# D's second projection units and A's units moved later in the mixer, with the conv's norm beside D's first half

## The chip, the cores and the metric

The kernel runs on one core of a Trainium2 chip. Its time is device time in microseconds of that core. Five engines work at once, each on its own queue in program order: TensorE (PE, with its weight loads PEld), VectorE (DVE), ScalarE (ACT), GpSimd (POOL) and SyncE (SP), which issues the transfers (DMA).

## The reference, cut to what matters

Two layers of a transformer block work on 512 latent tokens and, in layer 0, on 256 context tokens beside them (768 in all). Layer 1 gives out latents only. Each layer projects the normed tokens once, splits the columns into four groups, and computes:

```python
y_a = window_gqa(qa, ka, va, ka_c, va_c, sink)          # banded attention with a sink
y_b = conformer_conv(ub, conv_w, conv_b, conv_ln_g, conv_ln_b)   # conv of 31 taps, then layernorm and silu
y_c = diff_out(diff_attention_latent(qc, kc, vc, kc_c, vc_c, lam), subln_g, lambda_init)
y_d = neighbourhood_attn(qd, kd, vd, kd_c, vd_c, rpb)   # 2-D neighbourhood, with a bias
yx = jnp.concatenate([y_a, y_b, y_c, y_d], axis=-1) @ w_out
x = x + g1 * yx
x = x + g2 * swiglu(modulate(rmsnorm(x, norm2_g[l]), sh2, sc2), w_gate[l], w_up[l], w_down[l])
```

The shifts, scales and gates (`sh1` to `g2`) are six vectors of a layer, each a product of the conditioning with a part of `w_ada`. They are called ada vectors below, (layer, number); (1, 2) is the gate `g1` of layer 1. The context tokens of layer 0 go through the same groups among themselves.

## The kernel before

Every large product is made of three matmuls of split operands (`mm3`, L177 to L179: high by high, high by low, low by high), so a *unit* of 128 projected columns is 8 slices of the model width by 3 matmuls over 512 latent columns, and as many over 256 context columns where the group needs them. A unit's weights come by one load of 512 KB, ACT writes the high part (L142) and DVE the low part (L144).

The mixer of a layer (`layer`) is written as generators that hand out steps. `beside(main, side, nm, ns)` runs an attention half as main and spreads the steps of a side list between its steps, at a rate set by the two numbers; `mix2` and `chain` join lists; `take(g, n)` takes n steps of a list. From what is written, a scheduler of the framework makes each engine's queue, which runs in order. The attentions work by blocks of 128 queries: scores on TensorE (L630 and L631 for C and A, L794 for D) into one PSUM tile (`sc` or `sd`) that holds one block, a reduction on DVE (L662 for C, L805 for D, L855 for A), exponentials on ACT, for C a combining of two weights on DVE (L671), transposes of the weights on TensorE (L515, L516) and the product with the values (L621, L622). D's bias is written by POOL (L775).

The stages of a layer, in order:

- B's units, then the conv's taps on DVE (L880), which go on beside the stages that follow.
- C's first half, beside C's second queries and keys and D's first ones.
- C's second half, beside `d_rest`: D's second queries and keys (`proj_d(l, H, c1, 1)`), the rest of the taps, and D's two value units.
- D's first half, beside three of A's units (keys, values, first queries: `take(pa, 3)`).
- D's second half, beside `rest`: A's last unit (second queries), the release of the projection's input `hT`, the pool for `w_out`, A's mask, C's norm (`c_norm`) and the conv's layernorm (`conv_norm`: two transposes to rows per 128 tokens, statistics on DVE, a power on POOL, then transposes back and the silu).
- A, beside `more`: the first loads of `w_out` and the ada vector (l, 2), in layer 1 the ada vector first.

After the mixer come the product with `w_out` and the FFN, whose tiles hold TensorE for most of the time. In the FFN of layer 0 the ada vectors of later use are made beside it by a lazy list (`ada_half`): it loads 512 KB at a time, in pairs into two buffers (`araw`), and TensorE takes the loads in with small matmuls (L312). How many steps of that list run for each hidden tile f is a number in the loop (`for _ in range(10 if f < 1 else 2)`). A vector takes eight loads.

## Time and profile before

| | us |
|---|---|
| median of three runs (1778.98 to 1782.14) | 1779.81 |
| the profiled execution | 1780.37 |
| span of its profile | 1778.6 |
| TensorE busy | 1702.3 (96%) |
| VectorE busy | 935.1 (53%) |
| ScalarE busy | 584.9 (33%) |
| GpSimd busy | 205.8 (12%) |

The share of busy time is a mean over stages of different kinds: the FFN and the projections have TensorE full, the attention stages use all engines. So the profile is read by stage here, in stretches cut where a stage's first score reduction starts. In layer 0 the cuts stand at 109.9 us (C's first half), 197.1 (C's second), 266.1 (D's first), 300.0 (D's second), 339.0 (A) and 405.5 (first product with `w_out`); in layer 1 at 1123.6, 1185.3, 1236.5, 1274.8, 1293.2 and 1350.8. The row of a stretch gives its length, each engine's busy time in it with the number of instructions, the clock that TensorE was granted (1.00 is 2.4 GHz, 0.50 is 1.2), the mean busy share of the DMA engines and the bandwidth.

### The profile page before, as it was taken

What the parts mean: (1) busy time and instruction counts of PE and PEld (TensorE: products, weight loads), DVE (VectorE), ACT (ScalarE), POOL (GpSimd) and SP (SyncE); (2) the same over time, 40 slices, a digit from 0 to 9 for tenths busy, and PEclk for the clock granted to TensorE, in tenths of its full rate; (3) what the DMA queues carried; (4) which work ended last, traced back from release to release, by engine and by line L of the source; (5) the groups of instructions that cost most, each with busy time, mean ns of one, the idle gap of its engine ahead of it and who ended that gap; (6) DMA issues with size and microseconds to landing.
All of it is one profiled execution on the core that took longest, in us unless ns stands there. A gap on an engine that the chain in (4) does not pass through costs nothing.

```text
span 1778.6 us, 26995 instructions
## 1 busy us (share of the span) xinstructions
PE 1702.3 (96%) x11236; PEld 1413.5 (79%) x11236; DVE 935.1 (53%) x1548; ACT 584.9 (33%) x1048; POOL 205.8 (12%) x194
## 2 busy tenths in 40 slices
PE   6999999779999999999999999999988999999997
PEld 4888787557898888888888889878766888888886
DVE  5678875762452342423324258688565445354354
ACT  4225544562241112121121233454354422321221
POOL 1101113520000010000000010212440001000000
PEclk8999999888999999999999999999998999999999
DMA  9351122235155243242331212111225253432421
GB/s 323 83 170 36 36 57 68 72 91 180 44 164 173 85 120 109 70 123 95 97 97 37 86 69 71 49 48 35 90 62 178 73 177 95 119 90 76 119 71 48
DMA packets 187976, 172.78 MB, mean 97 GB/s; under 512 B 17878, under 2 KB 150478, under 8 KB 187726
## 3 DMA queue, kind: packets, MB, share of 16 engines
q1 hardware_dynamic: 187854, 171.06, 31.3%
q8 instruction: 88, 1.44, 0.3%
q14 instruction: 34, 0.28, 0.0%
HBM read 166.76 MB, written 4.52 MB: 96 GB/s over the span
## 4 chain that ended last, share of the span: by engine, by line
PE 85%; DVE 5%; DMA 4%; ACT 2%; SPq 1%; issue 1%; POOL 1%; POOLq 0%; DVEq 0%; ACTq 0%
PE ps L177 19%; PE ps L178 19%; PE ps L179 19%; PE pu L177 5%; PE pu L178 5%; PE pu L179 5%; PE sc L631 3%; PE pt L516 2%; PE pt L622 2%; PE ada L312 2%; SPq L98 1%; DMA wraw<-in_w_in 1%; PE pu L622 1%; DMA wraw<-in_w_gate 1%; PE ptd L516 1%
## 5 line engine op out<-in xcount | busy, mean ns | idle before, releaser
L178 PE MATMUL ps<-h,whi 128*128 128x512 f32 (+1 forms) x1104 | 382.5, 347 | 1.6 <-DVE h L144 1.6
L177 PE MATMUL ps<-h,whi 128*128 128x512 f32 (+1 forms) x1104 | 382.6, 349 | 0.9 <-DVE gt L985 0.9
L179 PE MATMUL ps<-h,wlo 128*128 128x512 f32 (+1 forms) x1104 | 381.9, 347 | 0.0
L142 ACT CAST whi<-wraw 128x1024 fp32r<-128x1024 f32 (+1 forms) x132 | 134.3, 1022 | 448.6 <-PE ps L178 250.6
L144 DVE TENSOR_TENSOR wlo<-wraw,whi 128x1024 fp32r<-128x1024 f32 (+1 forms) x116 | 139.2, 1203 | 186.4 <-ACT whi L142 185.3
L177 PEld LDWEIGHTS ps<-h,whi 128*128 128x128 f32 x1104 | 207.8, 189 | 30.0 <-issue 1.6
L178 PEld LDWEIGHTS ps<-h,whi 128*128 128x128 f32 x1104 | 209.0, 189 | 27.4 <-DVE h L144 2.0
L179 PEld LDWEIGHTS ps<-h,wlo 128*128 128x128 f32 x1104 | 208.8, 189 | 26.6 <-issue 0.6
L177 PE MATMUL ps<-wdhi,zh 128*128 128x512 f32 x440 | 171.4, 391 | 0.4 <-ACT ntmp L387 0.4
L178 PE MATMUL ps<-wdlo,zh 128*128 128x512 f32 x440 | 170.5, 389 | 0.0
L179 PE MATMUL ps<-wdhi,zl 128*128 128x512 f32 x440 | 169.9, 389 | 0.0
L985 DVE TENSOR_TENSOR gt<-ps,g 128x1024 f32<-128x1024 f32 x66 | 80.6, 1223 | 167.1 <-PE ps L179 161.7
L177 PE MATMUL pu<-hT,whi 128*128 128x512 f32 (+1 forms) x456 | 161.4, 354 | 1.1 <-ACT whi L142 0.5
L179 PE MATMUL pu<-hT,wlo 128*128 128x512 f32 (+1 forms) x456 | 159.9, 351 | 0.5 <-DVE wlo L144 0.5
L178 PE MATMUL pu<-hT,whi 128*128 128x512 f32 (+1 forms) x456 | 160.1, 351 | 0.0
L142 ACT CAST wdhi<-wraw 128x1024 fp32r<-128x1024 f32 x44 | 46.1, 1052 | 269.0 <-PE ps L179 177.8
L988 POOL TENSOR_TENSOR x<-x,gt 128x1024 f32<-128x1024 f32 x12 | 29.7, 2472 | 722.0 <-DVE gt L985 722.0
L1252 DVE TENSOR_TENSOR sg<-sg,ps 128x768 f32<-128x768 f32 (+1 forms) x44 | 36.1, 821 | 144.4 <-PE ps L179 142.8
L880 DVE SCALAR_TENSOR_TENSOR accd<-hp,wcol,accd 128x783 f32<-128x783 f32 (+1 forms) x116 | 107.8, 929 | 2.7 <-ACT accd L876 1.2
L177 PEld LDWEIGHTS pu<-hT,whi 128*128 128x128 f32 x456 | 85.9, 189 | 16.3 <-issue 1.9
L177 PEld LDWEIGHTS ps<-wdhi,zh 128*128 128x128 f32 x440 | 82.6, 188 | 19.2 <-issue 1.0
L179 PEld LDWEIGHTS pu<-hT,wlo 128*128 128x128 f32 x456 | 86.1, 189 | 13.1 <-issue 1.9
(260 smaller groups left out, 2709.6 us busy)
## 6 DMA issues: line engine op xcount, KB each, us to landing
araw<-in_w_ada SPq DMA_DIRECT2D x60, 512.0 KB
wraw<-in_w_gate SPq DMA_DIRECT2D x44, 512.0 KB
wraw<-in_w_up SPq DMA_DIRECT2D x44, 512.0 KB
wraw<-in_w_down SPq DMA_DIRECT2D x44, 512.0 KB
wraw<-in_w_in SPq DMA_DIRECT2D x40, 512.0 KB
wraw<-in_w_ada SPq DMA_DIRECT2D x20, 512.0 KB
wraw<-in_w_out SPq DMA_DIRECT2D x12, 512.0 KB
whi<-in_w_ada SPq DMA_DIRECT2D x8, 512.0 KB
```

The source lines that it names most:

```text
L142: nc.scalar.copy(hi, src)
L144: eng.tensor_tensor(lo, src, f32(hi), op=ALU.subtract)
L177: mm(out, st[0], mv[0], start=first, stop=False)
L178: mm(out, st[0], mv[1], start=False, stop=False)
L179: mm(out, st[1], mv[0], start=False, stop=last)
L312: nc.tensor.matmul(ps[32 * j:32 * j + 32, 0:P], self.cstat[:, k, :], raw[:, a * 512 + j * P:a * 512 + (j + 1) * P], start=(k == 0), stop=( ...
L516: self.nc.tensor.transpose(pt[:, (i - a) * P:(i - a + 1) * P], blocks[i], self.ident)
L622: self.burst_of([lambda i=i, j=j: nc.tensor.matmul(po[64 * j:64 * j + 64, 0:P], *parts[j][i], start=(i == n - 1), stop=(i == 0)) for i in ...
L631: return [lambda o=o, q=q[a][r], k=k[b][r], i=i: self.nc.tensor.matmul(o, q, k, start=(i == 0), stop=(i == 2)) for i, (a, b) in enumerate( ...
L880: nc.vector.scalar_tensor_tensor(acc[:, 0:w], hp[:, k:k + w], wc, acc[:, 0:w], op0=ALU.mult, op1=ALU.add)
L985: nc.vector.tensor_tensor(tmp, ps, g, op=ALU.mult)
L1252: nc.vector.tensor_tensor(sg, sg, pss[1][:, 0:W], op=ALU.mult)
```

## The change

D's second queries and keys leave `d_rest` and go beside D's first half, chained with the first of A's units (keys) and mixed with `conv_norm`, which leaves `rest`. A's values and first queries go beside D's second half (`rest`), A's second queries, with the release of `hT` and the pool for `w_out` behind them, beside A (`more`). The ada vector (1, 2) leaves layer 1's A and joins the list of layer 0's FFN, whose steps per hidden tile change from 10 to 6 for the first and from 2 to 1 or 2 for the others; a step now loads a pair at once, where it took two steps. The conv norm's rows use one tile in the buffer of C's values (`V`) in place of two of the `qk` buffers. The rates of the side lists change.

```diff
--- before.py
+++ after.py
@@ -304,7 +304,6 @@
             if self.lazy and not raws and kk % 2 == 0:
                 two = [self.ada_load(l, vec, h, kk + a) for a in range(2)]
                 yield 0.8
-                yield 0.8
             raw = raws[kk] if raws else two[kk % 2] if self.lazy else self.ada_load(l, vec, h, kk)
             for a in range(2):
                 k = 2 * kk + a
@@ -905,9 +904,9 @@
             rs = self.small(1, "brs", 4)
             nc.vector.tensor_scalar(rs, mv[:, 1:2], EPS, None, op0=ALU.add)
             self.pow_m05(rs, rs, 1)
-            if n % 3 == 0:
-                x3 = self.tl(pool, [P, NT], "qk", self.QKB)
-            xn = x3[:, n % 3 * 256:n % 3 * 256 + 256]
+            if n == 0:
+                x6 = self.tl(pool, [P, 6, 256], "V", 1)
+            xn = x6[:, n]
             nc.vector.tensor_scalar(xn, pt[:, 0:256], mv[:, 0:1], rs, op0=ALU.subtract, op1=ALU.mult)
             xns.append(xn)
             yield 1.0
@@ -1094,7 +1093,8 @@
         nq = 6 if cx else 4
 
         def d_rest():
-            yield from self.proj_d(l, H, c1, 1)
+            yield
+            yield
             for _ in tp:
                 pass
             self.cv.release()
@@ -1109,20 +1109,19 @@
                 yield
 
         def rest():
-            yield from pa
-            self.half = 0
-            hTp.release()
-            held["wop"] = self.pool("wo", "right")
+            yield from self.take(pa, 2)
             self.maska = self.tl(held["c2"], [P, 768], "mask")
             self.dma(self.maska[:, 0:640], t["maska"])
             yield from self.c_norm(l, c1)
-            yield from self.conv_norm(l, c1)
 
         def more():
+            yield from pa
+            hTp.release()
+            held["wop"] = self.pool("wo", "right")
             self.burst, self.ada_tag = 15, ("pu", "pt")[l]
             self.atags = [("wraw", 3, F32, self.wst), ("whi", 3, F32R, self.wst), ("wlo", 3, F32R, self.wst)]
-            both = [self.load_wo(l, wo, held["wop"], range(wa)), self.ada_gen([(l, 2)])]
-            yield from self.chain(*both[::-1 if l else 1])
+            yield from self.load_wo(l, wo, held["wop"], range(wa))
+            yield from self.ada_gen([] if l else [(0, 2)])
 
         self.half = 0
         self.beside(self.mix2(self.c_attn(l, 0), tp, 2, False),
@@ -1132,12 +1131,13 @@
         self.psum_push("e")
         dn = 10 if cx else 8
         pa = self.proj_a(l, H, c1)
-        self.beside(self.d_attn(l, held["c2"], 0), self.take(pa, 3), dn, 3)
-        self.beside(self.d_attn(l, held["c2"], 1), rest(), dn, 14 if cx else 9)
+        self.beside(self.d_attn(l, held["c2"], 0), self.mix2(self.chain(self.proj_d(l, H, c1, 1), self.take(pa, 1)),
+                                                                     self.conv_norm(l, c1), 4), dn, 3)
+        self.beside(self.d_attn(l, held["c2"], 1), rest(), dn, 5 if cx else 4)
         self.psum_pop()
         self.psum_push("c")
         self.pv_tag = "pu"
-        self.beside(self.chain(self.a_attn(l, 0), self.a_attn(l, 1)), more(), 2 * dn, 12)
+        self.beside(self.chain(self.a_attn(l, 0), self.a_attn(l, 1)), more(), 2 * dn, (13, 4)[l])
         wop = held["wop"]
         held["c2"].release()
         c1.release()
@@ -1228,7 +1228,7 @@
         W = NT if cx else SEQ
         fin = None
         self.atags, self.lazy = [("araw", 2 if cx else 3, F32, fp)], 1
-        adas = self.ada_gen([(0, 5), (1, 0), (1, 1), (1, 3), (1, 4)] if cx else [(1, 5)])
+        adas = self.ada_gen([(0, 5), (1, 0), (1, 1), (1, 2), (1, 3), (1, 4)] if cx else [(1, 5)])
         f0 = 0
         for part in (4, 2, 4, 4, 4, 4):
             fs = list(range(f0, f0 + part))
@@ -1258,7 +1258,7 @@
                 hi, lo = self.split_tiles(fp, "wd", 4)
                 self.split(hi, lo, raw)
                 wds.append((hi, lo))
-                for _ in range(10 if f < 1 else 2):
+                for _ in range(6 if f < 1 else 1 + f % 2):
                     next(adas, None)
             last = f0 == NF
             if last:
```

What this does to TensorE's queue shows at two places. In the rows, `sc` and `sd` are score tiles of C and D, `pt` and `ptd` with `ident,Pm` are transposes of attention weights, and `pu` with `hT` and `whi` or `wlo` is a projection unit; numbers behind names are buffers.

TensorE in C's second half of layer 0, behind the scores of a block late in the half, before:

```order
L631 MATMUL sc_2413<-qk_1500,qk_1296 128x256 x2
L177 MATMUL pu_2645<-hT_71_342,whi_2641 128x512
L178 MATMUL pu_2645<-hT_73_344,whi_2641 128x512
L179 MATMUL pu_2645<-hT_71_342,wlo_2642 128x512
L177 MATMUL pu_2645<-hT_71_342,whi_2641 128x512
L178 MATMUL pu_2645<-hT_73_344,whi_2641 128x512
L179 MATMUL pu_2645<-hT_71_342,wlo_2642 128x512
L177 MATMUL pu_2645<-hT_71_342,whi_2641 128x512
L516 MATMUL pt_2355<-ident_88,Pm_2336 128x128 x2
L178 MATMUL pu_2645<-hT_73_344,whi_2641 128x512
L516 MATMUL pt_2388<-ident_88,Pm_2375 128x128 x4
L179 MATMUL pu_2645<-hT_71_342,wlo_2642 128x512
```

The same half after:

```order
L515 MATMUL pt_2225<-ident_88,Pm_2212 128x128 x4
L515 MATMUL pt_2231<-ident_88,Pm_2212 128x128 x2
L630 MATMUL sc_2289<-qk_1500,qk_1295 128x512 x2
L630 MATMUL sc_2289<-qk_1501,qk_1295 128x512 x2
L630 MATMUL sc_2289<-qk_1500,qk_1296 128x512 x2
L630 MATMUL sc_2289<-qk_1500,qk_1295 128x256 x2
L630 MATMUL sc_2289<-qk_1501,qk_1295 128x256 x2
L630 MATMUL sc_2289<-qk_1500,qk_1296 128x256 x2
L515 MATMUL pt_2264<-ident_88,Pm_2251 128x128 x4
L515 MATMUL pt_2270<-ident_88,Pm_2251 128x128 x2
L630 MATMUL sc_2411<-qk_1500,qk_1295 128x512 x2
L630 MATMUL sc_2411<-qk_1501,qk_1295 128x512 x2
```

Before, the matmuls of a unit stand between a block's scores and the next transposes of weights; after, the next block's scores and transposes follow each other.

TensorE in D's second half of layer 0 (`rt` and `yC` are C's norm), before:

```order
L794 MATMUL sd_3589<-qk_2251,qk_2059 128x256 x2
L516 MATMUL ptd_3514<-ident_88,Pm_3505 128x128 x4
L794 MATMUL sd_3676<-qk_2251,qk_2058 128x256 x2
L794 MATMUL sd_3676<-qk_2252,qk_2058 128x256 x2
L794 MATMUL sd_3676<-qk_2251,qk_2059 128x256 x2
L794 MATMUL sd_3676<-qk_2251,qk_2058 128x256 x2
L794 MATMUL sd_3676<-qk_2252,qk_2058 128x256 x2
L794 MATMUL sd_3676<-qk_2251,qk_2059 128x256 x2
L516 MATMUL ptd_3562<-ident_88,Pm_3553 128x128 x4
L622 MATMUL pt_3579<-PT_3510,VD_2462 64x128
L516 MATMUL ptd_3611<-ident_88,Pm_3602 128x128 x4
L708 MATMUL pu_3440<-ident_88,rt_3430 128x128 x4
```

The same half after, where one of A's units ends and the next one starts:

```order
L179 MATMUL pu_3313<-hT_71_342,wlo_3309 128x256
L177 MATMUL pu_3313<-hT_71_342,whi_3308 128x256
L178 MATMUL pu_3313<-hT_73_344,whi_3308 128x256
L179 MATMUL pu_3313<-hT_71_342,wlo_3309 128x256
L515 MATMUL ptd_3423<-ident_88,Pm_3414 128x128 x2
L515 MATMUL pt_3366<-ident_88,rt_3362 128x128 x4
L515 MATMUL ptd_3423<-ident_88,Pm_3414 128x128 x2
L177 MATMUL pu_3441<-hT_70_341,whi_3433 128x512
L178 MATMUL pu_3441<-hT_72_343,whi_3433 128x512
L179 MATMUL pu_3441<-hT_70_341,wlo_3434 128x512
```

Before, the scores of a block are followed by the transposes and products of the one before it, and no unit stands there; after, two of A's units stand here behind each other, with four rows of transposes' work between them.

## Rows read from the trace of the kernel before

**Rows 1.** The page: busy time, share of the span, instructions of each engine.

```profile
PE 1702.3 (96%) x11236; PEld 1413.5 (79%) x11236; DVE 935.1 (53%) x1548; ACT 584.9 (33%) x1048; POOL 205.8 (12%) x194
```

**Rows 2.** Layer 0 by stage: length, engines' busy us, clock, DMA share, GB/s.

```profile
197.10:266.10 69.00, 68.76 (x502) 55.20 (x501) 52.23 (x117) 35.17 (x82) 8.02 (x13) 1.00 0.19 45
266.10:300.00 33.90, 33.90 (x267) 26.66 (x265) 18.89 (x53) 12.43 (x35) 13.46 (x20) 1.00 0.22 73
300.00:339.00 39.00, 32.68 (x269) 25.28 (x267) 25.75 (x62) 23.63 (x54) 14.90 (x11) 0.87 0.31 95
339.00:405.50 66.50, 49.46 (x531) 37.64 (x532) 42.95 (x132) 37.96 (x97) 21.33 (x22) 0.88 0.24 74
```

**Rows 3.** Layer 1 by stage, columns as in rows 2.

```profile
1185.30:1236.50 51.20, 51.20 (x392) 42.75 (x394) 45.37 (x89) 27.12 (x58) 5.59 (x9) 1.00 0.14 35
1236.50:1274.80 38.30, 36.91 (x279) 29.52 (x276) 18.16 (x44) 11.71 (x29) 13.88 (x22) 1.00 0.35 103
1274.80:1293.20 18.40, 16.28 (x157) 11.80 (x156) 13.84 (x38) 12.65 (x31) 13.35 (x14) 1.00 0.07 20
1293.20:1350.80 57.60, 44.96 (x492) 34.04 (x492) 36.36 (x102) 35.12 (x75) 20.59 (x21) 0.92 0.31 93
```

**Rows 4.** DVE lines, C's second half, layer 1: count, busy, mean ns, idle before.

```profile
L662 DVE CUSTOM_DVE_ANT_0 Pm<-sc,zcol 128x768 f32<-128x768 f32 x16 | 14.7, 954 | 6.5 <-PE sc L631 6.4
...
L671 DVE SCALAR_TENSOR_TENSOR Pm<-Pm,cf,Pm 128x768 f32<-128x768 f32 x8 | 8.1, 1017 | 0.2
```

**Rows 5.** TensorE's timeline in a unit: start us, length, instruction.

```profile
214.33 0.40 PE L177 MATMUL pu<-hT,whi 128*128 128x512 f32 x1
214.57 0.40 PE L178 MATMUL pu<-hT,whi 128*128 128x512 f32 x1
...
221.70 0.28 PE L177 MATMUL pu<-hT,whi 128*128 128x256 f32 x1
221.81 0.28 PE L178 MATMUL pu<-hT,whi 128*128 128x256 f32 x1
```

**Rows 6.** DVE's timeline: score reductions of blocks without a unit, layer 1's D.

```profile
1274.82 0.69 DVE L805 CUSTOM_DVE_ANT_1 Pm<-sd,dnb 128x512 f32<-128x512 f32 x1 [0.33 <-PE sd L794]
...
1279.78 0.68 DVE L805 CUSTOM_DVE_ANT_1 Pm<-sd,dnb 128x512 f32<-128x512 f32 x1
...
1283.74 0.69 DVE L805 CUSTOM_DVE_ANT_1 Pm<-sd,dnb 128x512 f32<-128x512 f32 x1 [0.96 <-PE sd L794]
```

**Rows 7.** The conv's norm in layer 0's A: lines of TensorE and POOL.

```profile
L919 PE MATMUL pu<-ident,qk 128*128 128x128 f32 x12 | 3.4, 437 | 2.3 <-DVE es L740 1.1 <-ACT yB L921 0.9 <-DVE qk L911 0.4
...
L900 PE MATMUL pu<-ident,yB 128*128 128x128 f32 x12 | 2.5, 289 | 2.1 <-DVE qk L911 1.6 <-DVE r L821 0.4
...
L122 POOL TENSOR_TENSOR brs<-brs,mhalf 128x1 f32<-128x1 f32 x6 | 3.4, 573 | 4.9 <-DVE brs L906 2.9 <-DVE ls L746 2.0
```

**Rows 8.** The conv's norm in layer 1's A: lines of TensorE.

```profile
L900 PE MATMUL pu<-ident,yB 128*128 128x128 f32 x8 | 1.6, 286 | 0.0
...
L919 PE MATMUL pu<-ident,qk 128*128 128x128 f32 x8 | 1.1, 280 | 0.0
```

**Rows 9.** Layer 1's A: ACT's timeline, TensorE's waits (total, times, longest).

```profile
1309.00 1.04 ACT L142 CAST wohi<-wraw 128x1024 fp32r<-128x1024 f32 x1 [3.03 <-DMA wraw<-in_w_out]
...
1315.70 1.04 ACT L142 CAST wohi<-wraw 128x1024 fp32r<-128x1024 f32 x1 [2.39 <-DMA wraw<-in_w_out]
...
PE pu L622 <- ACT yB L921: 2.0, 1, 2.0
```

**Rows 10.** TensorE's timeline in layer 0's FFN, at two ada loads.

```profile
542.32 1.08 PE L312 MATMUL ada<-araw,cstat 128*32 128x128 f32 x32
543.33 0.39 PE L177 MATMUL ps<-h,whi 128*128 128x256 f32 x1
```

**Rows 11.** Two stretches of D's second half, layer 0, columns as in rows 2.

```profile
310.60:317.40 6.80, 3.93 (x37) 2.55 (x38) 6.80 (x16) 4.81 (x10) 2.02 (x3) 1.00 0.77 227
317.40:327.60 10.20, 8.19 (x46) 6.50 (x45) 7.69 (x17) 6.84 (x15) 7.81 (x7) 0.50 0.47 157
```

## The prediction

> **What bounds the kernel now.** I read the page first: TensorE is busy for 96% of the span, VectorE (DVE) for 53% [rows 1]. A change that only moves TensorE's work can therefore win no more than the time in which TensorE idles, waits or runs slowly, and has to be read by stage. I cut both layers at the first score reduction of each stage that the change touches: C's second half, D's first half, D's second half, A [rows 2, 3]. The reader is to see two regimes. In C's second half and D's first half TensorE has no idle time to speak of (68.8 of 69.0 us and 33.9 of 33.9 in layer 0; 51.2 of 51.2 and 36.9 of 38.3 in layer 1), at the full clock. In D's second half and A it idles: 6.3 + 17.0 us in layer 0, 2.1 + 12.6 in layer 1, and the granted clock averages 0.87, 0.88 and 0.92 in three of these four stretches. That is where projection units could fill holes, and the change moves them there. The other side: in C's second half VectorE is itself busy for 52.2 of 69.0 us and for 45.4 of 51.2, and its score reductions there also stand 6.5 us for the scores [rows 4]. It has little to give when the units leave.
>
> **Price of what moves.** Within a unit the matmuls of 512 columns start 0.24 us apart and those of 256 columns 0.12 [rows 5]. A unit over latents and context is 24 of each, 24 x 0.237 + 24 x 0.118 = 8.5 us; over latents alone, as D's and A's queries are in layer 1, 5.7. By the change's order of TensorE's work, projection matmuls priced so come to, in layer 0: the end of C's first half +5.5, C's second half 39.9 before and 11.6 after, D's first half 16.4 and 8.5, D's second half 3.6 and 25.6, A 0 and 8.5. In layer 1: -2.1, then 29.3 and 14.6, 20.3 and 8.5, 0 and 22.7, 0 and 5.7. The sums agree: nothing is added here, it is all a move.
>
> **Layer 0, step by step.** C's first half: of the 5.5 us that are pulled forward into its last blocks, most fill slack of blocks that VectorE holds; I take +1.5 (bounds 0 and 5.5). C's second half: TensorE would be left with 68.8 - 28.3 = 40.5 us, VectorE with nearly its 52.2, so VectorE or the chain from score to weight sets the pace. The stage has twelve blocks, 69.0 / 12 = 5.75 us each now with 3.3 us of units; the three that keep units hold 3.9 of them, so 6.2 each (18.7 in all). Four blocks over latents and context without units I estimate at 4.8 us (two reductions of 0.95 and a combining step of 1.02 [rows 4]; the other 1.9 for a conv tap, small steps and waits), one with three more taps of about 1 us at 7.8, four over context, with a third of the columns, at 3.65. That is 60.3, so -8.7; the floor is 52.2 and the ceiling 69.0. D's first half: a block without a unit is read from layer 1's D, where reductions of successive blocks start 4.96 and 3.96 us apart [rows 6]; I take 4.3. Four such blocks, and one with the unit (4.0 + 8.5): 29.7, so -4.2. D's second half: layer 1's shows the work of four blocks, 16.3 us [rows 3], so five are 20.4; with units of 25.6 and 3.5 of the 6.3 us that TensorE idled before: 49.5, so +10.5. The units have their weights loaded and split by ACT and DVE long before, and the buffers rotate; the load runs in a stretch where DMA is at 0.31 [rows 2]. A: the norm's transposes go (3.4 + 2.5 us, with 2.3 + 2.1 waited ahead of them [rows 7]: 10.3) and a unit comes (8.5): -1.8. Sum of layer 0: 1.5 - 8.7 - 4.2 + 10.5 - 1.8 = -2.7.
>
> The conv norm goes beside D's first half and costs nothing there in this sum: its 5.9 us of TensorE lie in blocks that have become bare, and its DVE work beside DVE's 18.9 of 33.9. What could uncover it is POOL, whose powers of 0.57 us [rows 7] now stand ahead of D's bias: at worst 6 x 0.57 = 3.4 us in layer 0, 4 x 0.57 = 2.3 in layer 1, if each bias is waited for.
>
> **Layer 1, step by step.** C's first half: -2.2, since the pulled work shrinks by 2.1. C's second half: TensorE 51.2 - 14.7 = 36.5, but DVE's 45.4 stay and so do most of its waits; 50.0, so -1.2 (floor 45.4). D's first half: three bare blocks at 4.3 and one with the unit (4.5 + 8.5) are 25.9, so -12.4. D's second half: its 16.3 us of work and 22.7 of units, 39.0, so +20.6: this stretch had only 2.1 us of idle to fill. A: ACT stands 3.0 and 2.4 us for w_out, whose loads are queued behind the eight ada loads [rows 9]; with the ada vector gone these 5.4 us go. The norm's last wait of 2.0 goes [rows 9]; of TensorE's work the norm (1.6 + 1.1 [rows 8]) and the ada matmuls (4.0, below) go and a unit of 5.7 comes, -1.0. Together -8.4. Sum of layer 1: -2.2 - 1.2 - 12.4 + 20.6 - 8.4 = -3.6.
>
> **FFN of layer 0.** The eight loads of the vector now arrive beside matmuls that keep TensorE full. Two loads' worth of ada matmuls hold it for 1.01 us, from 542.32 to 543.33 [rows 10]; four such are +4.0. Three loads for each hidden tile in place of two on average: if the two buffers were late, each pair could wait, 0 to 4 us; I take 0.
>
> **Sum.** -2.7 - 3.6 + 4.0 = -2.3 us against the profiled execution's 1780.4, so 1778.1; that execution lies 0.6 above the median of the runs, so 1777.5 on their scale, rounded down to 1777. The parts are ten times the sum (-38.9 and +36.6), so the sum's sign is weak.
>
> **A rule against the change.** The rows say that C's second half holds TensorE and DVE full at once, as units of the one lie in the waits of the other [rows 2 to 4]. The Trainium skill, Perfetto Trace Analysis, section Optimization Strategy, says that regimes with different most-contended engines may gain from being interleaved. Pulling the units out of C's tail undoes such an interleaving, and putting them into D's second half makes one there; by that rule the sign hangs on which stretch had more idle time, which the sums above weigh.
>
> **Rivals.** *Slower, by the clock.* After a stretch in which TensorE was busy for 3.9 of 6.8 us the granted clock fell to 0.50 for the next 10.2 us [rows 11], the lower of its two levels, 1.2 GHz. The change leaves bare the rest of C's second half and D's first blocks: some 59 us in layer 0 (60.3 - 18.7 + 17.2) and 37 in layer 1. If they lose what A's bare stretch loses now, 12% and 8% of it by its mean clock of 0.88 and 0.92 [rows 2, 3], that is 7.1 + 3.0 = 10 us, and up to 4 more where the first unit begins at the lower clock (2 in each layer): +10 to +14, against -2.3: about 1788. It decides as soon as the bare blocks lie at the lower level for over 5 us or so. For it: the same kind of blocks in A do it. Against it: C's blocks have more TensorE work than A's. The Trainium skill, TensorE: Matmul & The Clock Gate, section A second HAM failure mode: psum-queue depth-cycling, describes a clock that goes back and forth when TensorE idles briefly between groups while it cycles PSUM; C's and D's one score tile each would be such a place.
>
> *Faster, by the same clock.* With units in D's second half and A the lower levels there vanish: A would get back up to 12% of 66.5 and 8% of 57.6 us, 8.0 + 4.6 = 12.6, beyond the sum (D's second half is already priced at the full clock): about 1765. For it: a unit is 8.5 us of unbroken matmuls. Against it: A's unit stands at its second and third block, and the low stretches come later.
>
> *It does not do what it says.* In layer 0 the order leaves D's second queries early beside C; were the keys to follow, little would be left but the FFN's +4.0 and A's stalls, -5.4: about 1779.
>
> **How the numbers follow.** A measurement of this kernel can tell about 0.2% (3.6 us) from no change. The forecast (small terms cancel, 1770 to 1784) has a chance of 0.40: 0.17 faster by more than that, 0.19 within, 0.04 slower, as DVE's floors in C would let it fall and the FFN's waits rise. The slower rival has 0.34 (0.29 slower, 0.05 within), the faster one 0.22, all faster; the last 0.04, within. That is 0.39 faster, 0.28 same, 0.33 slower. Since cases of both signs hold most of the chance, the range takes in both rivals: 1762 to 1792.
>
> **What would show it.** C's second half at 60 and 50 us, or nearer 52 and 45; D's first half at 30 and 26; D's second half at 50 and 39 with TensorE all busy; the FFN 4 us longer. A granted clock under 1 in C's second half or D's first half shows the slower rival; a clock of 1 all through A the faster one. I am wrong if C's bare blocks take over 6 us each, or if D's bias or the ada buffers become what TensorE waits for.

## The result and the profile after

The changed kernel took 1808.39 us (median; 1807.61 to 1812.72), the kernel before 1779.39 us in the same runs: a ratio of 1.0166, with an interval of 1.0151 to 1.018. It is slower by 29 us. 1777 was forecast, and the range ended at 1792.

The page of the changed kernel (busy time of each engine, then the chain that ended last by engine; the kernel before is in [rows 1]):

```profile
PE 1717.5 (95%) x11236; PEld 1424.3 (79%) x11236; DVE 938.6 (52%) x1548; ACT 582.8 (32%) x1048; POOL 206.0 (11%) x194
...
PE 83%; DVE 7%; DMA 4%; ACT 3%; SPq 2%; issue 1%; POOL 1%; DVEq 0%; POOLq 0%; ACTq 0%
```

The number of TensorE's instructions is the same. The span grew from 1778.6 to 1805.8 us, by 27.2. The stages of both layers after, cut as in [rows 2, 3], but A up to the first product with `w_out` (in the kernel before layer 0's stands at 406.5 us, and not at the 405.5 of [rows 2], so its A took 67.5; the columns are length, busy us of PE, PEld, DVE, ACT and POOL, the granted clock, DMA share, GB/s); the first five rows are layer 0's C first half, C second half, D first half, D second half and A, the next five layer 1's:

```profile
110.20:199.90 89.70, 89.55 (x672) 73.23 (x671) 69.64 (x132) 42.61 (x92) 15.40 (x6) 1.00 0.23 66
199.90:259.30 59.40, 50.12 (x385) 39.78 (x385) 50.33 (x117) 31.06 (x76) 9.44 (x15) 0.86 0.14 32
259.30:286.80 27.50, 26.06 (x216) 20.36 (x215) 20.53 (x59) 12.66 (x36) 14.60 (x23) 1.00 0.08 18
286.80:342.10 55.30, 52.43 (x392) 42.09 (x391) 26.33 (x68) 24.08 (x61) 12.73 (x12) 0.97 0.19 58
342.10:414.50 72.40, 57.94 (x579) 44.37 (x579) 46.78 (x120) 41.08 (x101) 19.77 (x17) 0.93 0.38 119
1135.50:1195.10 59.60, 59.60 (x401) 47.45 (x402) 45.73 (x84) 31.78 (x62) 12.22 (x5) 1.00 0.18 54
1195.10:1250.10 55.00, 46.64 (x326) 37.34 (x326) 47.80 (x91) 25.90 (x55) 8.41 (x10) 0.81 0.16 41
1250.10:1283.30 33.20, 26.60 (x205) 21.13 (x204) 17.45 (x49) 12.13 (x29) 17.80 (x29) 0.90 0.10 20
1283.30:1324.20 40.90, 40.55 (x298) 32.56 (x299) 17.93 (x47) 16.19 (x39) 9.81 (x9) 1.00 0.10 27
1324.20:1375.80 51.60, 43.02 (x363) 32.25 (x358) 33.32 (x87) 32.70 (x72) 20.32 (x17) 0.93 0.24 72
```

The reader is to see three things. C's second half has lost TensorE's load: 50.1 of 59.4 us and 46.6 of 55.0, where it was full before [rows 2, 3]. D's second half is where the time went: 39.0 to 55.3 us and 18.4 to 40.9, with TensorE busy for nearly all of it. And the granted clock is below 1 where it was 1.00 before, in C's second half of both layers and in D's first half of layer 1.

The sums of these ten stretches, before and after (length, then busy us of each engine):

```profile
sum 523.80, PE 483.16 PEld 382.92 DVE 371.40 ACT 272.57 POOL 141.15; mean PE 48.32 PEld 38.29 DVE 37.14 ACT 27.26 POOL 14.11
```

```profile
sum 544.60, PE 492.51 PEld 390.57 DVE 375.82 ACT 270.19 POOL 140.51; mean PE 49.25 PEld 39.06 DVE 37.58 ACT 27.02 POOL 14.05
```

The mixers are 20.8 us longer: 9.3 us of TensorE's busy time and 11.5 of its idle time. About 5 more of the 27.2 lie in layer 0's FFN: the stretch from its first matmul to layer 1's C, which holds layer 1's first units too, went from 643.7 to 649.1 us:

```profile
486.40:1135.50 649.10, 646.23 (x4236) 556.30 (x4234) 270.08 (x301) 151.23 (x183) 29.06 (x19) 1.00 0.33 102
```

### The profile page after: what moved, and what is told of

Its sections match the earlier page's. It is cut to its first block, busy times and chain, and to the rows that moved or that the text cites. A ratio compares the mean times of both kernels' runs of the same rounds, so it can differ in the third digit from the quotient of the medians.

```text
span 1805.8 us, 27028 instructions
## 1 busy us (share of the span) xinstructions
PE 1717.5 (95%) x11236; PEld 1424.3 (79%) x11236; DVE 938.6 (52%) x1548; ACT 582.8 (32%) x1048; POOL 206.0 (11%) x194
## 4 chain that ended last, share of the span: by engine, by line
PE 83%; DVE 7%; DMA 4%; ACT 3%; SPq 2%; issue 1%; POOL 1%; DVEq 0%; POOLq 0%; ACTq 0%
PE ps L177 19%; PE ps L178 19%; PE ps L179 18%; PE pu L177 5%; PE pu L178 5%; PE pu L179 5%; PE sc L630 2%; PE pt L621 2%; PE pt L515 2%; SPq L98 2%; PE ada L311 2%; DMA wraw<-in_w_in 1%; DVE accd L879 1%; DVE Pm L661 1%; PE pu L621 1%
## 5 line engine op out<-in xcount | busy, mean ns | idle before, releaser
L144 DVE TENSOR_TENSOR wlo<-wraw,whi 128x1024 fp32r<-128x1024 f32 (+1 forms) x116 | 137.2, 1186 | 202.0 <-ACT whi L142 200.9
```

The lines of the kernel that those rows point to most:

```text
L144: eng.tensor_tensor(lo, src, f32(hi), op=ALU.subtract)
```

## Where no unit runs: the conv's norm in TensorE's order

TensorE's timeline after, layer 0, the norm's transposes (L899 here is L900 before) and the first matmul of a unit behind them:

```profile
221.03 0.33 PE L899 MATMUL pu<-ident,yB 128*128 128x128 f32 x1
221.63 0.27 PE L899 MATMUL pu<-ident,yB 128*128 128x128 f32 x1
244.89 0.44 PE L899 MATMUL pu<-ident,yB 128*128 128x128 f32 x2
...
273.08 0.51 PE L177 MATMUL pu<-hT,whi 128*128 128x512 f32 x1
```

DVE's timeline beside it: the conv's last taps (L883), and the write of the norm's rows into the buffer of C's values; then TensorE's last product that reads C's values:

```profile
244.09 1.15 DVE L883 SCALAR_TENSOR_TENSOR yB<-hp,wcol,accd 128x512 f32<-128x512 f32 x2
...
265.07 0.99 DVE L910 TENSOR_SCALAR V<-pu,bmv,brs 128x256 f32<-128x256 f32 x2
```

```profile
263.88 0.65 PE L621 MATMUL pt<-PT,V 128*64 128x128 f32 x6
```

The norm and the projection units share one ring of PSUM tiles (`pu`, in the kernel's table of tiles 512 columns wide, two of them; a ring is a set of buffers that are used in turn), and tiles of a ring are handed out in program order. In the changed kernel the program has the norm's first four steps, each with a tile, ahead of D's second keys. TensorE takes the first tile at 221.0 us and the second at 221.6, each for the half of the channels whose taps are done. The other half follows at 244.9, behind the first of the last taps; the statistics are ready at about 250, but the rows are to be written into the buffer of C's values, which C reads until 264.5. So both tiles are held for 44 us, from 221.0 to 265.1; then the norm's next two steps take them, and TensorE runs no matmul of a unit from 218.0 to 273.1. In layer 1 the tiles are held from 1218.9 to 1262.6, and the next unit comes at 1270.9. That suggested the first theory: it is this ring that makes C's tail bare and pushes the units into D's second half. The rival was that the places written for the units cost by themselves.

## The experiments

Stage lengths in us, from the score reductions in each run's trace (C1, C2: C's halves; D1, D2: D's; A up to the first `w_out` product), the sum for a layer's mixer, and the median:

| kernel | layer 0: C1 C2 D1 D2 A | sum | layer 1: C1 C2 D1 D2 A | sum | us |
|---|---|---|---|---|---|
| before | 87.2 69.1 33.8 39.0 67.5 | 296.6 | 61.7 51.2 38.3 18.4 57.6 | 227.2 | 1779.4 |
| after | 89.7 59.4 27.6 55.3 72.3 | 304.3 | 59.5 55.0 33.2 40.8 51.7 | 240.2 | 1808.4 |
| x1, norm back | 89.7 72.1 26.2 25.7 82.2 | 295.9 | 59.5 60.7 25.4 20.2 58.8 | 224.6 | 1781.6 |
| y2, norm behind units | 89.7 65.9 22.1 45.8 68.9 | 292.4 | 59.5 60.5 23.4 29.8 48.6 | 221.8 | 1776.4 |
| y1, D's units back | 87.2 64.6 21.5 45.7 69.2 | 288.2 | 61.7 51.2 24.7 32.7 49.0 | 219.3 | 1772.5 |
| w1, norm in ptd | 89.7 64.4 41.8 34.3 69.3 | 299.5 | 59.5 59.3 19.8 31.5 49.4 | 219.5 | 1783.7 |
| z1, norm in qk | 89.6 62.1 36.8 45.2 70.7 | 304.4 | 59.5 55.6 40.9 30.7 53.5 | 240.2 | 1804.6 |
| x2, norm alone | 87.2 64.5 31.6 50.5 57.5 | 291.3 | 61.7 51.2 40.7 22.6 53.9 | 230.1 | 1778.0 |
| x3, ada alone | 87.2 69.0 33.8 39.1 67.2 | 296.3 | 61.7 51.2 38.1 18.3 43.0 | 212.3 | 1771.2 |
| z2, D's units alone | 89.7 71.9 29.0 34.8 67.9 | 293.3 | 59.5 60.5 31.0 21.5 48.4 | 220.9 | 1778.5 |
| y4, A's last unit | 87.2 69.1 30.8 23.5 78.5 | 289.1 | 61.7 51.2 34.7 17.7 54.3 | 219.6 | 1773.0 |

Between kernels with the same text for layer 1's mixer (x3, y3, z3, w2) its A alone ran from 43.0 to 47.3 us, so single stages of A are told apart here by 5 us and no finer. Beside x3, which has only the ada part, the changed kernel's mixer is 8.0 us longer in layer 0 and 27.9 in layer 1: most of what the moves cost lies in layer 1.

### The norm back in its place, and the norm alone

```diff
-        ..., self.mix2(self.chain(self.proj_d(l, H, c1, 1), self.take(pa, 1)), self.conv_norm(l, c1), 4), dn, 3)
+        ..., self.chain(self.proj_d(l, H, c1, 1), self.take(pa, 1)), dn, 3)
             yield from self.c_norm(l, c1)
+            yield from self.conv_norm(l, c1)
```

> The changed kernel with the conv norm back behind C's norm, beside D's second half, in its qk buffers; all else as changed. Theory 1: the norm, put ahead of the units in the ring of two projection PSUM tiles (pu), holds both tiles from C's second half on until C's values leave their buffer, so that no unit can start there; that alone makes C's tail bare and bunches the units in D's second half. By its order the units then stand beside C's second half again (36.6 us of unit matmuls in layer 0 in place of 11.6, 36.5 in layer 1 in place of 14.7). It expects layer 1's D stages together to lose over 20 us against the changed kernel, the clock to stay at 1.00 in C's second half, and a time of 1775 to 1786. Theory 2: what costs is the places that were written for the units (D's second ones beside D, A's last beside A); it expects 1795 or more.

1781.56 us, 1.0008 (0.9999 to 1.0018) of the kernel before: 27 us of the 29 are gone, though all units keep the places that the change gives them in the lists. Layer 1's two D stages fell from 74.0 to 45.6 us, and the clock in C's second half is back (0.98 and 1.00). Theory 1 held. The text above says `qk` buffers, but the edit leaves the norm's rows in the buffer of C's values (in the trace, DVE writes `V` from 331.0 us on); only the norm's place changed.

The second run takes the kernel before and moves the norm only:

```diff
+                x6 = self.tl(pool, [P, 6, 256], "V", 1)
...
-            yield from self.conv_norm(l, c1)
...
-        self.beside(self.d_attn(l, held["c2"], 0), self.take(pa, 3), dn, 3)
+        self.beside(self.d_attn(l, held["c2"], 0), self.mix2(self.take(pa, 3), self.conv_norm(l, c1), 4), dn, 3)
```

> The kernel before with one edit: the conv norm beside D's first half, in the buffer of C's values, mixed with A's three units; D's second units stay beside C. Theory 1 (the norm holds the two pu tiles): slower than before by 5 to 15 us, since no unit's matmuls stand in the last two blocks of C's second half and the first four of D's in layer 0, and the three units come back to back in blocks 5 to 7 of D. Theory 2 (the places of the units): the norm fills holes and leaves A, 0 to -10 us.

1777.97 us, 0.9991 (0.9981 to 1.0). Here theory 1's number missed: 5 to 15 us slower was expected, and it is even. The units do stand late, and D's second half of layer 0 grew by 11.5 us, but C's second half lost 4.6 and A, without the norm, 10.0. Here D's second units are ahead of the norm in the ring, and its first transposes stand at 255.4 us, 6 us before C's second half ends. So the norm ahead of A's units is not dear by itself. With D's units moved behind it as well it is: 27 us.

### The order in the list, and the ring alone

```diff
-        ..., self.mix2(self.chain(self.proj_d(l, H, c1, 1), self.take(pa, 1)), self.conv_norm(l, c1), 4), dn, 3)
+        ..., self.chain(self.proj_d(l, H, c1, 1), self.take(pa, 1), self.conv_norm(l, c1)), dn, 13)
```

> The changed kernel with the norm behind the three units of D's first half's list and not mixed between them, so that its tiles come after theirs in the pu ring; the same places otherwise. Theory 1 expects the units to be pulled into C's second half (28.7 us in layer 0, 31.8 in layer 1 by the order) and most of the loss to go: 1776 to 1788, as with the norm moved back (1781.6). If the norm's own work beside D (POOL's powers ahead of D's bias, DVE) is what costs, it stays above 1795.

1776.39 us, 0.9976 (0.9966 to 0.9987). The same work beside the same stage, in another order in one list, is 32 us faster than the changed kernel. The stages of C's second half, D's first half and D's second half in this run, layer 0 and then layer 1 (columns as above):

```profile
199.50:265.40 65.90, 63.65 (x481) 50.62 (x481) 53.87 (x122) 34.73 (x84) 8.71 (x14) 0.97 0.13 30
265.40:287.50 22.10, 17.62 (x163) 12.72 (x164) 20.87 (x62) 10.31 (x30) 15.10 (x23) 1.00 0.26 67
287.50:333.30 45.80, 42.68 (x347) 34.22 (x347) 21.39 (x60) 22.57 (x58) 12.83 (x12) 1.00 0.15 47
...
1183.40:1243.90 60.50, 57.52 (x424) 46.75 (x424) 51.88 (x96) 29.39 (x63) 8.43 (x10) 1.00 0.15 38
1243.90:1267.30 23.40, 20.83 (x163) 15.77 (x164) 17.13 (x51) 10.95 (x26) 15.55 (x24) 0.85 0.24 57
1267.30:1297.10 29.80, 28.31 (x225) 22.12 (x225) 13.45 (x37) 13.25 (x33) 11.96 (x14) 1.00 0.04 12
```

Against the changed kernel, 17.1 us of unit matmuls stand in C's second half instead of D's stages, by the order of either layer. C's second half pays 6.5 and 5.5 us for them; D's two stages save 15.0 and 20.8. So a unit beside C, where TensorE had 9.3 and 8.4 us to spare, cost a third of its length; beside D the stages shrank by 0.9 and 1.2 of it. These are differences of whole stages: the norm's place and the granted clock differ between the two kernels as well, so not all of them need be the units'.

The last run of this question changes the ring only, at both places where the norm takes a tile; program, place and buffers stay:

```diff
     def conv_norm(self, l, pool):
...
-            pt = self.ps('pu')
+            pt = self.ps('ptd')
```

> The changed kernel with one edit: the conv norm takes its PSUM tiles from the ring of D's transposes (ptd), which exists only in D's stages, in place of the ring of the projection units (pu). Place, order of the lists and buffers stay as changed. Theory 1 (the ring that norm and units share) expects nearly the whole loss to go: by the order 28.7 and 31.8 us of unit matmuls stand in C's second half (11.6 and 14.7 in the changed kernel), and the time is 1766 to 1780. If what decides is that the norm stands ahead of the units in the list, by whatever tile, or its work beside D, it stays at 1795 or more.

1783.74 us, 1.0018 (1.0009 to 1.0027). 25 us of the 29 are gone, a little less than expected (1766 to 1780). Its stages, C's second half and D's halves of layer 0, then of layer 1:

```profile
199.60:264.00 64.40, 62.72 (x470) 50.43 (x471) 51.85 (x116) 34.67 (x83) 8.23 (x13) 0.97 0.13 30
264.00:305.80 41.80, 32.55 (x225) 23.84 (x224) 24.16 (x72) 14.43 (x38) 16.56 (x26) 0.80 0.15 38
305.80:340.10 34.30, 33.68 (x298) 26.84 (x299) 18.70 (x55) 18.85 (x52) 11.52 (x10) 1.00 0.18 62
1190.30:1249.60 59.30, 58.80 (x431) 48.00 (x432) 50.48 (x97) 29.37 (x63) 8.61 (x10) 1.00 0.15 39
1249.60:1269.40 19.80, 18.42 (x166) 14.12 (x165) 13.66 (x44) 8.11 (x22) 13.32 (x23) 1.00 0.29 67
1269.40:1300.90 31.50, 27.72 (x224) 20.80 (x221) 20.48 (x44) 16.12 (x38) 16.05 (x18) 1.00 0.04 11
```

In layer 1, where D's transposes use another ring (`pt`), the mixer is down to 219.5 us, 20.7 less than in the changed kernel and as short as in y1 below. In layer 0 D's transposes use `ptd` too, and the norm now stands in their way: D's first half took 41.8 us with 9.3 of TensorE idle, most of it behind the norm's rows (total, times, longest):

```profile
PE ptd L918 <- DVE V L910: 5.0, 2, 4.6
PE ptd L899 <- DVE V L910: 2.1, 1, 2.1
```

So the cause is the shared ring, and it is not tied to `pu`: in both rings tried, the norm's waits became those of the work behind it. One limit: the `ptd` ring comes later in the program, so in this run the norm also starts later (269.3 us in layer 0, 1245.1 in layer 1); no run has an early norm in a ring of its own.

### Which wait of the norm, and D's units back

Two smaller cuts. The norm's rows in the `qk` buffers again, all else as changed:

```diff
-                x6 = self.tl(pool, [P, 6, 256], "V", 1)
...
+                x3 = self.tl(pool, [P, NT], "qk", self.QKB)
...
```

> The changed kernel with the norm's rows in two qk buffers, as before, in place of the buffer of C's values; place and order as changed. It tells the two waits of the norm apart. In the trace of the changed kernel its first two pu tiles are taken at 221.0 and 221.6 us, wait for the last taps (243.3) and then for C's last product to leave the values' buffer (265.1). If the second wait matters, units start in the first blocks of D (17.1 us of unit matmuls in D's first half in each layer, by the order, in place of 8.5): 5 to 15 us off 1808, 1793 to 1803. If the first wait or the ring's order alone decides, 1803 to 1810.

1804.64 us, 1.0146 (1.0127 to 1.0165): 4 us of 29, less than what a wait for the values' buffer should have given. The units did move within D, D's first half grew by 9 and 8 us and the second fell by 10 and 10. The sums of the mixers are those of the changed kernel (304.4 and 240.2 us), so even the 4 us do not lie there. The buffer is not the cause.

D's second units back beside C, the norm left ahead of A's keys:

```diff
         def d_rest():
-            yield
-            yield
+            yield from self.proj_d(l, H, c1, 1)
...
-        ..., self.mix2(self.chain(self.proj_d(l, H, c1, 1), self.take(pa, 1)), self.conv_norm(l, c1), 4), dn, 3)
+        ..., self.mix2(self.take(pa, 1), self.conv_norm(l, c1), 4), dn, 3)
```

> The changed kernel with D's second queries and keys back beside C's second half; the norm stays beside D's first half, A's units and the ada part stay as changed. Theory 1 (the norm holds both pu tiles, and what it costs is the number of units that stand behind it in that ring while C runs): with D's keys no longer behind it, C's second half is covered again (29.3 us of unit matmuls in layer 1, clock 1.00, 51 us in place of 55.0), D's second half in layer 1 falls from 40.8 to about 30; 1776 to 1788. Theory 2 (the two units of A in D's second half and the third in A are what costs): the gain is under 10 us, 1799 or more.

1772.45 us, 0.9954 (0.9939 to 0.9969), 36 us faster than the changed kernel and better than expected (1776 to 1788). With D's keys ahead of it in the ring, the norm's first transposes in layer 0 stand only at 255.9 us, 6 us before C's second half ends, and C is covered: 51.2 us in layer 1, as before.

### The other parts alone

The ada part, with the changed steps of its list (cut here):

```diff
-        adas = self.ada_gen([(0, 5), (1, 0), (1, 1), (1, 3), (1, 4)] if cx else [(1, 5)])
+        adas = self.ada_gen([(0, 5), (1, 0), (1, 1), (1, 2), (1, 3), (1, 4)] if cx else [(1, 5)])
...
-            both = [..., self.ada_gen([(l, 2)])]
+            both = [..., self.ada_gen([] if l else [(0, 2)])]
```

> The kernel before with the ada part alone: layer 1's vector (1, 2) made beside layer 0's FFN, with the changed steps. From the two traces: the FFN of layer 0 took 5.4 us more, and the waits of ScalarE for w_out in layer 1's A (3.0 and 2.4 us) should go, with 4 us of ada matmuls: sum -4 to +2, so 1775 to 1782. If the sum is +4 or more, the stalls for w_out were hidden behind another wait.

1771.19 us, 0.9947 (0.9931 to 0.9964), below the expected 1775 to 1782: it gains 8.5 us. The FFN took 5.1 us more, but layer 1's A fell from 57.6 to 43.0 us. ACT's casts of the `w_out` rows in this run, which had stood 3.0 and 2.4 us in [rows 9]:

```profile
1337.45 1.04 ACT L142 CAST wohi<-wraw 128x1024 fp32r<-128x1024 f32 x1 [0.86 <-DMA wraw<-in_w_out]
1339.52 1.04 ACT L142 CAST wohi<-wraw 128x1024 fp32r<-128x1024 f32 x1 [0.86 <-DMA wraw<-in_w_out]
```

The two moves of units alone, each on top of the ada part:

```diff
         def d_rest():
-            yield from self.proj_d(l, H, c1, 1)
+            yield
+            yield
-        self.beside(self.d_attn(l, held["c2"], 0), self.take(pa, 3), dn, 3)
+        self.beside(self.d_attn(l, held["c2"], 0), self.chain(self.proj_d(l, H, c1, 1), self.take(pa, 1)), dn, 3)
```

> The kernel before with the ada part and the move of D's second units (then A's keys) beside D's first half; norm and A's other units beside D's second half. Theory 1: without the norm ahead of them the units are pulled into C's second half by the scheduler as before (36.6 and 36.5 us of unit matmuls there), so the move alone is nearly nothing: 1771.2 +- 4. Theory 2: the move costs by itself, 1780 or more.

1778.53 us, so +7.3 against 1771.2 (+8.5 if each is set against the kernel before in its own group of runs, 1778.6 and 1779.7), between the two theories. The scheduler pulls units into C's second half as before. In layer 0 the move is even (293.3 against 296.3 us in x3). In layer 1 C's second half holds 36.5 us of unit matmuls by the order, 29.3 before, and is 9.3 us longer; D's two halves together give back 3.9. So a unit beside C is not cheap once TensorE is full there: 7.2 us more of them cost 9.3. Part of that is DVE's: the same 19 taps of the conv take 18.0 us there in place of 14.4 (see the last section).

```diff
         def rest():
-            yield from pa
...
         def more():
+            yield from pa
...
```

> The kernel before with the ada part and A's last unit (second queries, with the release of the input's buffers and the pool for w_out) moved from D's second half to A. The prediction charged such a unit with its own 8.5 us in layer 0 and 5.7 in layer 1 in A, and as much less in D's stages: 0 +- 3 us against 1771.2. The trace of the changed kernel, where layer 1's A took 51.7 us against 43.0 with the ada part alone, though it had no norm any more, speaks for more: the unit stands in TensorE's queue ahead of products that wait on nothing, so A grows by its whole length and D gains little: +5 to +12, 1776 to 1783.

1772.97 us, +1.8: within what the prediction had charged, and less than the trace of the changed kernel had made me expect. But it is a sum of two misses. A grew by 11.3 us in either layer, where 8.5 and 5.7 had been charged; D's stages gave back 18.6 us in layer 0 and 4.0 in layer 1. Layer 0 gained 7.2 us and layer 1 lost 7.3.

So the parts add up as: ada -8.5, the moves of units with the norm where it was +10.4 (x1 against x3; by the table all of it in layer 1; +7.3 and +1.8 for the two moves one by one), and the norm ahead of D's keys in the ring +26.8 (the changed kernel against x1), in all +28.7.

### TensorE's clock

The slower rival of the prediction said that the lower clock in the bare blocks would be the loss. Two kernels add transposes whose results nobody reads behind the weights of these blocks:

```diff
+                if u and n >= 2:
+                    self.fill(Pm[1], 12, "pt")
...
+                if not u and g < 3:
+                    self.fill(S, 8, self.tr_tag)
```

> The changed kernel with extra transposes whose results nobody reads: 12 behind each weight block of C's second half from its third query block on, 8 behind each of D's first half up to the third. They keep TensorE at work in the bare blocks. If the lower clock is what makes these blocks long in layer 1 (0.81 in C's second half, 55.0 us, and 0.90 in D's first half, 33.2 us), the clock rises to 1.00 there and the two stretches fall from 88.2 to 80 us or less, though there is more to do. If the chain from score to weight sets their pace at any clock, they stay at 88 or grow by up to 15 us.

1811.92 us, 1.0179 (1.0154 to 1.0203); the two runs took 1808.6 and 1815.2, so it can't be told from the changed kernel. C's second half and D's first half together: 97.1 us in layer 0 (87.0 without) and 88.5 in layer 1 (88.2), the clock still below 1 in C's second half (0.90 and 0.85). In D's first half of layer 1 it is back at 1.00, and this stretch alone was 30.5 us in place of 33.2. Nothing was decided, so more of it:

> As x4_fill with 28 extra transposes behind each weight block of C's second half and 12 behind each of D's first half. In x4_fill, 17.9 us more of TensorE's work made the profiled run 7.7 us longer, and the lower clock covered 48 us of the mixers in place of 68. If the clock was worth half of what it covers, the clock is now 1.00 in C's second half of both layers and that stage stays at or under 65 and 58 us although it has some 10 and 5 us more to do. If the chain sets the pace, it grows by what is added.

1829.73 us, 1.0286 (1.0262 to 1.0309). C's second half and D's first half of layer 0, then C's second half of layer 1:

```profile
199.40:267.20 67.80, 64.25 (x563) 54.82 (x563) 50.68 (x117) 31.69 (x77) 9.25 (x15) 0.97 0.13 31
267.20:304.80 37.60, 37.60 (x333) 32.59 (x331) 20.65 (x64) 11.84 (x33) 15.74 (x24) 1.00 0.04 10
...
1209.20:1269.00 59.80, 55.19 (x396) 45.52 (x397) 48.17 (x92) 26.27 (x56) 11.14 (x16) 0.86 0.17 41
```

In layer 0 the clock is back (0.97 and 1.00, from 0.86 in C), TensorE is busy for 25.7 us more, and the two stretches are 18.5 us longer. A faster clock gave nothing back that shows, but nor can a gain be excluded under that much more work. In layer 1's C the clock did not come back (0.86), and its D's first half, at 1.00, took 34.7 us with this filler and 30.5 with the smaller one, against 33.2 at 0.90: there it stays open. A bound: the mixers' busy time on TensorE grew by 9.3 us for work that had lost about 4 us of ada matmuls, so over all ten stretches the lower clock can have cost some 13 us more of TensorE's busy time than before at most. The runs that bring the units back beside C bring back the clock too, so how much of the 27 to 32 us that the norm's place costs goes through the clock is not shown.

### What was built on it

> The kernel before with the ada part (1771.2 alone) and the norm beside D's first half in layer 0 only. In the run of the norm alone layer 0's mixer stages came to 291.3 us against 296.6 before, layer 1's to 230.1 against 227.2, so the sum should be 1771.2 - 5.3 = 1766, 1763 to 1769.

1768.58 us, 0.9931 (0.9913 to 0.9948).

> The ada part in both layers; in layer 0 the norm beside D's first half with A's keys, A's values and first queries beside D's second half and A's last unit beside A; layer 1's mixer as before. Stages from two runs: layer 0 as in y1_d_units_back (288.2 us against 290.1 in y3_ada_and_norm_l0), layer 1 as in x3_ffn_alone: 1764 to 1769.

1766.42 us, 0.9934 (0.9917 to 0.9951), the lowest median of all: layer 0 as in y1, layer 1's mixer as before, and the ada part. It beats both kernels; from y3 it can't be told apart.

> z3_l0_moved (1766.4) with the norm of layer 0 in ptd. A's keys then stand beside C (39.8 us of unit matmuls in C's second half in place of 34.1) and its values and queries are spread over D: 1758 to 1768.

1779.71 us, 0.9996 (0.9986 to 1.0006): it missed the expected range by 11.7 us. As in w1, the norm in D's own ring costs D's first half of layer 0 (45.8 us in place of 21.3).

## Why the prediction was wrong, step by step

| stage | forecast | measured |
|---|---|---|
| layer 0: C1, C2 | +1.5, -8.7 | +2.5, -9.6 |
| layer 0: D1, D2 | -4.2, +10.5 | -6.4, +16.3 |
| layer 0: A | -1.8 | +4.9 |
| layer 1: C1, C2 | -2.2, -1.2 | -2.1, +3.8 |
| layer 1: D1, D2 | -12.4, +20.6 | -5.1, +22.5 |
| layer 1: A | -8.4 | -6.0 |
| FFN of layer 0 | +4.0 | +5.4 |

The step that failed is the sentence that "the conv norm goes beside D's first half and costs nothing there in this sum". Put where the change puts it, ahead of D's keys in the ring that it shares with the units, the norm costs 26.8 us (the changed kernel against x1) to 32.0 (against y2). In y2 it runs beside D's first half too, so the fault is the order in the ring and not the stage. I priced its matmuls and POOL's powers, and did not ask which tiles it takes, who is behind it in that ring, and what it waits for before it gives them back. I had the consequence before me: the order of TensorE's work showed that C's tail had lost the units, and I counted 28.3 us of matmuls leaving it. I took that for the written move itself. The run x1 shows that with the same written places the units stay in C's tail. Reading the order told me where they stood, not why.

The bare tail was thus in the sum, by the positions, and with the positions known the sum should still have come out near. It had -2.3 us; the table's measured column adds up to +26.2. The terms that were too kind are D's first half in layer 1 (by 7.3 us), A in layer 0 (6.7), D's second half in layer 0 (5.8), C's second half in layer 1 (5.0), A and D's second half in layer 1 (2.4 and 1.9), the FFN (1.4) and C's first halves (1.1); two were 2.2 and 0.9 too harsh. Taking 28.3 and 14.7 us of units out of C's second halves changed these by -9.6 and +3.8 us.

D's second half of layer 0 has 52.4 - 25.6 = 26.8 us of other work on TensorE, where I scaled layer 1's 16.3 us to 20.4; the norm's second transposes lie there too (from 289.2 us on). Layer 1's C second half has more DVE work than before (47.8 us against 45.4) and a granted clock of 0.81; I had taken 50.0. What each of the two is worth is not shown. In layer 1's D first half the first two blocks took 7.0 and 7.1 us, where I had taken 4.3 for a bare block, and the one with the unit 15.0, where I had 13.0. A part of that I had put in the bounds only: DVE's waits in the stretch 1245 to 1262, where POOL's powers stand between the two biases (total, times, longest; the wait for the bias was 1.6 us in D's first half before):

```profile
DVE Pm L804 <- POOL dnb L774: 3.7, 2, 2.8
DVE r L820 <- ACT Pm L807: 1.2, 2, 0.9
```

In A of layer 0 the unit took 10.6 us (350.8 to 361.4) in place of 8.5: for its first 4.3 us the granted clock was 0.50. And TensorE waits longer for the transposed attention weights that ACT copies, 5.4 us where it was 2.0 before:

```profile
PE pu L621 <- ACT PT L526: 5.4, 4, 1.9
PE pu L707 <- DVE rt L701: 1.7, 2, 1.3
```

C's second half of layer 0 was right to 1 us, as were the first halves of C. The FFN's term was mis-sized by 1.4: four pairs of loads cost 5.4 us, not 4.0; the ada buffers were hardly waited for, as assumed.

Layer 1's A came near by two errors that cancel in part. The ada vector's removal is worth 14.6 us there by itself in x3, where I summed 5.4 of ACT's waits and 4.0 of matmuls; but the unit made A some 11 us longer in y4 (told apart to 5 us only), where I charged 5.7.

Two of the prediction's signs of being wrong came, both in layer 1: the five blocks of C's second half that the held ring left bare took 6.4 us each in the mean (1218.0 to 1250.1), and D's bias became what DVE waited for (3.7 us). One small slip in its working: the blocks that keep units, 5.75 - 3.3 + 3.9, are 6.3 us each and not 6.2, 0.3 us in the sum.

The slower rival had the side right, and its rows came (0.86, 0.81 and 0.90 in just the stretches it named), but it ended at 1788, and filling the stretches did not show the clock to be the loss. The rule of the Trainium skill (Perfetto Trace Analysis, section Optimization Strategy), that regimes with different most-contended engines may gain from being interleaved, agrees with the rows of y2 above: 17.1 us of units cost 6.5 and 5.5 us in C's second half, where TensorE had idle time and DVE was as busy (50.1 and 50.3 us of 59.4 in layer 0 of the changed kernel), and 15.0 and 20.8 in D's stages, where TensorE is busy nearly all of the second half.

## What to carry to other kernels

Before a step is moved ahead of others in program order, list the rings of tiles that it shares with them, and what it waits for before it frees them: work behind it in the ring waits too, even on an engine that is idle. An order of instructions that looks different from what was written is a finding to explain, not only a place to price. And filler work belongs in the stages that another engine paces: here a unit of TensorE's work cost a third of its length beside C, as long as TensorE had idle time there, and about its whole length beside D.

## What the runs showed that I had not expected

Eight loads of 512 KB and 4 us of small matmuls taken out of layer 1's A made this stage 10 to 15 us shorter (57.6 us before, 43.0 to 47.3 in the four runs with the same text there). Bringing the granted clock from 0.86 to 0.97 in C's second half of layer 0 by filling did not make that half shorter, with 14.1 us more of busy time in it.

Two taps of the conv in layer 1's C second half took 2.90 and 2.43 us in place of 0.75. Each ran beside one of POOL's splits of a weight (L144) and ended 0.54 us after it. The second of them:

```profile
1219.22 2.38 POOL L144 TENSOR_TENSOR wlo<-wraw,whi 128x1024 fp32r<-128x1024 f32 x1 [20.03 <-ACT PT L526]
1219.71 2.43 DVE L879 SCALAR_TENSOR_TENSOR accd<-hp,wcol,accd 128x512 f32<-128x512 f32 x1
```

The 19 taps of that half, before and after (busy us, mean ns, idle before):

```profile
L880 DVE SCALAR_TENSOR_TENSOR accd<-hp,wcol,accd 128x512 f32<-128x512 f32 x19 | 14.4, 760 | 0.2
...
L879 DVE SCALAR_TENSOR_TENSOR accd<-hp,wcol,accd 128x512 f32<-128x512 f32 x19 | 18.1, 951 | 0.2
```

The taps take 18.0 us there in x1, y2, z2 and w1 too, all kernels in which D's second units left `d_rest`, and 14.4 in x3, y1 and z3, in which they did not. One such tap stood in C's first half before, so over both halves it is 2 us more.
